# A two-layer decoder trunk on one core: SwiGLU's first stage by 256 gate and 256 up features, two steps of mLSTM's head 0 on other engines, and one early DMA on another queue

## The chip, the cores and the metric

The kernel runs on one core of a Trainium2 chip. The metric is the device time of one launch in microseconds (us). Before the change it is 825.69 us, the median of 3 runs (825.42 to 826.16). The engines are named as in the profile: PE multiplies matrices, DVE and POOL work elementwise, ACT copies, casts and evaluates functions, and SP issues DMAs (so does ACT's queue, for one of them).

## The reference, cut to what matters

256 tokens, model width 1024, two layers. Layer i is a token mixer (gMLP for layer 0, mLSTM with 4 heads of 512 for layer 1), then SwiGLU, then a sigmoid-gated embedding. All of it is float32.

```
def swiglu(x, w_gate, w_up, w_down):           # 1024 -> 2816 -> 1024
    return (jax.nn.silu(x @ w_gate) * (x @ w_up)) @ w_down

# mLSTM, per head: P = (q k^T) * decay weights, lower triangular; num = P v; den = sum P
h = layer_norm(num / max(|den|, exp(-m)), norm_g) + skip * xc
return (h * jax.nn.silu(z)) @ w_out

x = layer_norm(ALPHA * x + mixer(x), ln1_g[i], ln1_b[i])
x = layer_norm(ALPHA * x + swiglu(x, ...), ln2_g[i], ln2_b[i])
x = x + sigmoid(x @ ple_w_gate[i] + ple_b_gate[i]) * (p[i] @ ple_w_proj[i])
```

## The kernel before

**Weights and products.** The weights are streamed from HBM in tiles of 512 KB (`raw`, 4 buffers, issued by SP at L176). `split` (L153) makes of each a high part, a cast by ACT, and a low part, a subtraction by DVE. The two parts of a weight stand in a tile `w` (6 buffers) or, for the keys in `WIDE`, in a tile of the pool `b8` (8 buffers); those in `EARLY` are split some blocks ahead of their use. A product is three matmuls: high by high, high by low, low by high. A planner puts the instructions of each engine in an order of its own, and waits follow from the data; PSUM is used as two rings of four banks, A and B.

**SwiGLU** (`channel_mixer`). The 2816 hidden features are 22 blocks of 128. For blocks 0 to 3 the tokens are the stationary operand: `first(t)` (L537) fills, for token tile t of 128 tokens, one bank with 512 gate features and one with 512 up features, 24 matmuls of 512 columns each (16 at L286/L287, 8 at L289). ACT and DVE make `hn` of them (L552, L553), which `transpose_h` (L560) turns into feature order by four transposes a tile and splits into `hs`. Between the gate bank and the up bank of token tile 0 stand the eight transposes of the second token tile of x (`transpose_x(1)`, L326), after which ACT and DVE split `xs` for that tile. Blocks 4 to 21 go by `gate_up(f)` (L567): the weights are stationary, high matmuls take x's high and low part side by side (512 columns, L260), low ones 256 columns (L264). `down_blocks` says after which f which blocks are multiplied by the down weights (12 matmuls a block, `acc`, L240 to L242): 0 to 3 after f = 5, then one a step.

**mLSTM's heads.** P of a head (`sc`, 128 x 384, L917) is split in two: `phi` by ACT, `plo` by POOL (L920, with `sub=pool`). `pv_block` (L925) multiplies them by v (L937 to L939, L939 with `plo`) and sums P's rows (`pd`); DVE then takes the row scale and the statistics (`dn`, `hst`, `hmv`, `hrs`), POOL a power (L962), and ACT writes the normalised head `hn` (L967). `h_block` (L973) transposes it, adds the skip (L980), multiplies by silu(z) (`y*sz`, L981, DVE) and splits the result into `hs`. The output product `acc` starts with blocks 0 to 2 on token tile 0 (four banks A), then on token tile 1, whose banks are those that held head 3's `num` until L967 has read them.

**The start.** x arrives transposed, in four tiles `xr` (L359 to L368). The first half of the first tile is issued by ACT's queue, its second half by SP, between the two halves of the first weight tile (L178). The first six matmuls (L422) need the first half of `raw`, those after them the second, which ACT casts at L382.

Of the kernel before, what the change touches and what calls it, by code (L numbers as in the profile page):

```python
# [9 lines left out]
F32R = mybir.dt.float32r  # L10
# [4 lines left out]
P = 128  # L15
# [31 lines left out]

WIDE = {(n, l, k) for l in range(2) for n, m in (("g", 4), ("u", 2), ("pg", 6)) for k in range(m)}  # L50
EARLY = {("wo", 17 + k): ("g", 0, k) for k in range(4)}
EARLY |= {("mo", 8 + 2 * k): ("g", 1, k) for k in range(3)}
EARLY |= {("d", l, 10 + k): ("pg", l, k) for l in range(2) for k in range(6)}


def down_blocks(f):

    return range(4) if f == 3 + LAG else [f - LAG] if f > 3 + LAG else []

# [2 lines left out]

def stationary(key):

    return key[0] in ("u", "xm") and len(key) == 2 or key[0] in ("g", "u", "z") and key[-1] >= 4


def paired(key):  # L70

    return key[0] in ("g", "u") and len(key) == 3 and key[-1] >= 4 or key[0] == "u" and len(key) == 2


def weight_plan(a):
# [16 lines left out]

    def ffn(l):
        add(("pj", l, 0), a["ple_proj"][l, 0])
        for n in ("g", "u"):
            for kp in range(4):
                add((n, l, kp), a["ffn_" + n][l, kp])
        for f in range(4, NF + LAG):
            for n in ("g", "u") if f < NF else ():
                add((n, l, f), a["ffn_" + n][l, f])  # L100
# [33 lines left out]
def trunk(ctx, tc, a, out):  # L134
# [35 lines left out]
    def ahead(loads, casts):  # L170
        while at["load"] < min(len(plan), at["use"] + loads):
            ap = plan[at["load"]][1]
            n = ap.shape[-1]
            t = tl("raw", [P, n], name="raw")
            for c in HALF if at["load"] < 3 else [slice(0, n)]:
                at["dma"] = sp.dma_start(t[:, c], ap[:, c])  # L176
                if at["load"] == 0 and c.start == 0:
                    second_x()  # L178
            raws[at["load"]] = t
            at["load"] += 1  # L180
        while at["cast"] < min(len(plan), at["use"] + casts):
# [177 lines left out]
    for i in range(4):  # L359
        t = tl("m2", [P, 2, S], name="xr")  # L360
        if i == 0:

            act.dma_start(t[:, 0, :], a["xT"][i, :, 0, :])
            second_x = lambda: sp.dma_start(xr[0][:, 1, :], a["xT"][0, :, 1, :])
            xr.append(t)
        else:
            sp.dma_start(t, a["xT"][i])
            xr.append(t)  # L368
        ahead(1 + i, 0)
# [147 lines left out]
    def channel_mixer(l, acc, last, hook=None):  # L517
# [19 lines left out]

        fw = {}  # L540

        def first(t, between=lambda: None):
            ps = {}
            for n in ("g", "u"):
                if t == 0:
                    fw[n] = [weight(n, l, kp) for kp in range(4)]
                ps[n] = bank("B", [P, 512], "first")
                tok_from_x(ps[n], t, fw[n])
                if n == "g":
                    between()  # L550
            h = tl("m2", [P, 512], name="hn")
            act.activation(h, ps["g"], AF.Silu)  # L552
            dve.tensor_tensor(h, h, ps["u"], ALU.mult)  # L553
            return h

        hn = [first(0, lambda: transpose_x(1)), first(1)]
        hs = {e: tl("h", [P, 2, S], F32R, "h") for e in range(4)}

        def transpose_h(t):
            tp = bank("B", [P, 4, P], "tp")  # L560
            for e in range(4):
                pe.transpose(tp[:, e, :], hn[t][:, e * P:(e + 1) * P], ident)
            for e in range(4):
                split(hs[e][:, 0, TOK[t]], hs[e][:, 1, TOK[t]], tp[:, e, :])

        def gate_up(f):
# [20 lines left out]

        transpose_h(0)
        rows = []
        for f in range(4, NF + LAG):  # L590
            if f < NF:
                gate_up(f)
            if f == 4:
                transpose_h(1)
                acc = Down(NF)
            for e in down_blocks(f):
# [105 lines left out]
    def mlstm(embed1):  # L702
# [156 lines left out]
        with tc.manual_schedule(engines={mybir.EngineType.Activation}):  # L859
# [43 lines left out]
            for h in range(NH):  # L903
# [67 lines left out]
        def h_block(h):  # L971
            for j in range(2):
# [43 lines left out]
def lay_out(inputs):  # L1016
# [26 lines left out]
    def part(w):  # L1043
# [14 lines left out]
        "ffn_g": np.stack([mixed(w) for w in i["ffn_w_gate"]]),  # L1058
        "ffn_u": np.stack([mixed(w) for w in i["ffn_w_up"]]),
# [44 lines left out]
```

## Time and profile before

| what | value |
|---|---|
| median of 3 runs | 825.69 us |
| profiled execution, its own time | 825.63 us |
| its span | 823.9 us |
| PE busy | 816.9 us (99%) |
| DVE, ACT, POOL busy | 75%, 57%, 18% |
| granted TensorE clock | 1.00 of full speed |
| DMA read | 153.67 MB |

All times below are of the one profiled execution and count from the start of its span; 1.7 us of its time lie outside the span. The granted clock is 1.00 throughout, the level of 2.4 GHz. A row of the timeline gives the start, the duration, the engine, the line, the operation with the tiles it writes and reads, and, in brackets, how long the engine sat idle before it and what released it. Ends of PE's matmuls are modelled, so that the pace of PE is read from starts.

### The profile page before, as it was taken

To read this page: it belongs to the slowest core of one execution; us is meant where nothing else is said; L and a number is where in the kernel's file an instruction comes from. 1 tells how busy PE (TensorE), PEld (TensorE's weight loads), DVE (VectorE), ACT (ScalarE), POOL (GpSimd) and SP (SyncE) were. 2 spreads that over 40 slices of the span, in tenths; PEclk is the share of its full clock that TensorE was granted. 3 is DMA by queue.
4 is the path that set the end of the run, shared out by engine and by line. 5 is a ranking of instruction groups with operands and counts; after the bars stand their busy time and mean duration, and the time that the engine had idled before them with its cause. 6 is when DMAs were issued, how large, how long until landed. Compare 5 with 4: busy or idle time off the path is not lost.

```text
span 823.9 us, 12407 instructions
## 1 busy us (share of the span) xinstructions
PE 816.9 (99%) x4520; PEld 708.0 (86%) x4520; DVE 614.3 (75%) x982; ACT 470.9 (57%) x820; POOL 149.6 (18%) x209
## 2 busy tenths in 40 slices
PE   9999999999999999999999999999999999999997
PEld 6888888888888888888889999988888888888886
DVE  6757998678956567586878998889885656776674
ACT  6656666565535556475256788776444555665522
POOL 1020643342000000700001677330000000000000
PEclk9999999999999999999999999999999999999999
DMA  8895447567176678677144355454626667886501
GB/s 287 283 337 182 153 159 225 179 194 243 67 260 202 192 225 281 201 229 252 38 146 156 135 162 161 146 177 147 215 90 224 196 199 228 269 264 212 179 1 51
DMA packets 44997, 155.52 MB, mean 189 GB/s; under 512 B 5256, under 2 KB 6024, under 8 KB 44936
## 3 DMA queue, kind: packets, MB, share of 16 engines
q1 hardware_dynamic: 44792, 154.60, 57.6%
q8 instruction: 35, 0.57, 0.3%
q14 instruction: 26, 0.21, 0.1%
q10 hardware_dynamic: 144, 0.13, 0.0%
HBM read 153.67 MB, written 1.05 MB: 188 GB/s over the span
## 4 chain that ended last, share of the span: by engine, by line
PE 96%; DVE 1%; ACT 1%; DMA 1%; issue 0%; POOL 0%; SPq 0%; DVEq 0%; ACTq 0%
PE acc L240 9%; PE acc L241 9%; PE acc L242 9%; PE pu L260 8%; PE pg L260 8%; PE ups L260 5%; PE pg L264 4%; PE pu L264 4%; PE ups L264 3%; PE vps L242 2%; PE vps L240 2%; PE vps L241 2%; PE xmps L245 2%; PE xmps L247 2%; PE xmps L246 2%; PE gate L289 2%
## 5 line engine op out<-in xcount | busy, mean ns | idle before, releaser
L153 DVE TENSOR_TENSOR w<-raw,w 128x1024 fp32r<-128x1024 f32 (+1 forms) x275 | 333.2, 1219 | 74.7 <-ACT w L153 73.1
L153 ACT CAST w<-raw 128x1024 fp32r<-128x1024 f32 (+1 forms) x275 | 284.9, 1046 | 120.6 <-PE acc L242 25.7
L240 PE MATMUL acc<-w,h 128*128 128x512 f32 x336 | 133.0, 396 | 0.2 <-ACT hn L967 0.2
L241 PE MATMUL acc<-w,h 128*128 128x512 f32 x336 | 131.3, 391 | 0.0
L242 PE MATMUL acc<-w,h 128*128 128x512 f32 x336 | 131.0, 390 | 0.0
L242 PEld LDWEIGHTS acc<-w,h 128*128 128x128 f32 x336 | 63.1, 188 | 13.9
L240 PEld LDWEIGHTS acc<-w,h 128*128 128x128 f32 x336 | 63.1, 188 | 12.1 <-ACT hn L967 0.6
L241 PEld LDWEIGHTS acc<-w,h 128*128 128x128 f32 x336 | 63.1, 188 | 11.2 <-DVE h L153 0.2
L260 PE MATMUL pg<-xs,w 128*128 128x512 f32 x288 | 71.6, 391 | 0.0
L260 PE MATMUL pu<-xs,w 128*128 128x512 f32 x288 | 71.5, 390 | 0.0
L260 PEld LDWEIGHTS pg<-xs,w 128*128 128x128 f32 x288 | 53.8, 188 | 11.0
L260 PEld LDWEIGHTS pu<-xs,w 128*128 128x128 f32 x288 | 53.8, 188 | 11.0
L319 POOL TENSOR_TENSOR rs<-ve,mhalf 128x1 f32<-128x1 f32 x8 | 7.6, 956 | 295.9 <-DVE ve L318 291.3
L271 ACT COPY s<-pg 128x256 f32<-128x256 f32 x36 | 13.4, 372 | 69.7 <-PE pg L264 69.7
L260 PE MATMUL ups<-xs,w 128*128 128x512 f32 x192 | 47.9, 391 | 0.0
L272 DVE TENSOR_TENSOR s<-s,pg 128x256 f32<-128x256 f32 x36 | 15.1, 421 | 42.8 <-ACT s L271 42.7
L260 PEld LDWEIGHTS ups<-xs,w 128*128 128x128 f32 x192 | 35.7, 188 | 7.2
L264 PEld LDWEIGHTS pg<-xs,w 128*128 128x128 f32 x288 | 38.9, 188 | 3.1
L264 PE MATMUL pg<-xs,w 128*128 128x256 f32 x288 | 39.5, 280 | 0.0
L264 PE MATMUL pu<-xs,w 128*128 128x256 f32 x288 | 39.4, 279 | 0.0
L264 PEld LDWEIGHTS pu<-xs,w 128*128 128x128 f32 x288 | 36.5, 188 | 0.3
L245 PE MATMUL xmps<-xs,w 128*128 128x256 f32 x128 | 36.3, 284 | 0.0
(252 smaller groups left out, 1635.7 us busy)
## 6 DMA issues: line engine op xcount, KB each, us to landing
raw<-in_ffn_g SPq DMA_DIRECT2D x44, 512.0 KB, 4.4
raw<-in_ffn_u SPq DMA_DIRECT2D x44, 512.0 KB, 4.6
raw<-in_ffn_d SPq DMA_DIRECT2D x44, 512.0 KB, 4.3
raw<-in_gm_u SPq DMA_DIRECT2D x24, 512.0 KB, 3.5
raw<-in_gm_wo SPq DMA_DIRECT2D x24, 512.0 KB, 3.4
raw<-in_gm_v SPq DMA_DIRECT2D x21, 512.0 KB, 5.2
raw<-in_ple_gate SPq DMA_DIRECT2D x16, 512.0 KB, 4.5
raw<-in_ml_z SPq DMA_DIRECT2D x16, 512.0 KB, 3.8
```

Source lines behind the costliest of these rows:

```text
L153: return dve.tensor_copy(hi, src) if fast else act.copy(hi, src), sub.tensor_tensor(lo, src, hi.bitcast(F32), ALU.subtract)
L240: pe.matmul(ps, lh, w[:, 0, c], start=start, stop=False)
L241: pe.matmul(ps, ll, w[:, 0, c], start=False, stop=False)
L242: pe.matmul(ps, lh, w[:, 1, c], start=False, stop=stop)
L245: pe.matmul(ps, w[:, 0, c], h, start=start, stop=False)
L246: pe.matmul(ps, w[:, 0, c], l, start=False, stop=False)
L247: pe.matmul(ps, w[:, 1, c], h, start=False, stop=stop)
L260: pe.matmul(ps, w[:, 0, k * P:(k + 1) * P], xs[:, k], start=k == 0, stop=False)
L264: pe.matmul(ps[:, 0], w[:, 1, k * P:(k + 1) * P], xh[:, k, :], start=False, stop=k == KD - 1)
L271: act.copy(o, ps[:, 1])
L272: dve.tensor_tensor(o, o, ps[:, 0], ALU.add)
L289: pe.matmul(ps, xl[:, k, TOK[t]], w[:, 0, c], start=False, stop=k == KD - 1)
```

## The change

Five places change. (1) `first(t)` fills one bank with 256 gate and 256 up features, from four new weight tiles `f` per layer that hold both side by side; so it covers blocks 0 and 1, and `gate_up` takes 2 to 21. `transpose_x(1)` stands between the high matmuls and the low ones of token tile 0. (2) Down blocks 0 and 1 come together after f = 3, then one a step. (3) `plo` of head 0 is DVE's, those of heads 1 to 3 stay POOL's. (4) The gate `y*sz` of head 0's four blocks is POOL's, those of the other heads stay DVE's. (5) Both halves of x's first tile are issued by ACT's queue.

```diff
-WIDE = {(n, l, k) for l in range(2) for n, m in (("g", 4), ("u", 2), ("pg", 6)) for k in range(m)}
-EARLY = {("wo", 17 + k): ("g", 0, k) for k in range(4)}
-EARLY |= {("mo", 8 + 2 * k): ("g", 1, k) for k in range(3)}
+WIDE = {(n, l, k) for l in range(2) for n, m in (("f", 4), ("pg", 6)) for k in range(m)}
+EARLY = {("wo", 17 + k): ("f", 0, k) for k in range(4)}
+EARLY |= {("mo", 8 + 2 * k): ("f", 1, k) for k in range(4)}
...
 def down_blocks(f):
-    return range(4) if f == 3 + LAG else [f - LAG] if f > 3 + LAG else []
+    return range(2) if f == 1 + LAG else [f - LAG] if f > 1 + LAG else []
...
-                if at["load"] == 0 and c.start == 0:
-                    second_x()
...
-            act.dma_start(t[:, 0, :], a["xT"][i, :, 0, :])
-            second_x = lambda: sp.dma_start(xr[0][:, 1, :], a["xT"][0, :, 1, :])
+            for k in range(2):
+                act.dma_start(t[:, k, :], a["xT"][i, :, k, :])
...
-        def first(t, between=lambda: None):
-            ps = {}
-            for n in ("g", "u"):
-                if t == 0:
-                    fw[n] = [weight(n, l, kp) for kp in range(4)]
-                ps[n] = bank("B", [P, 512], "first")
-                tok_from_x(ps[n], t, fw[n])
-                if n == "g":
-                    between()
+        def first(t, before=(None, None)):
+            if t == 0:
+                fw.extend(weight("f", l, kp) for kp in range(4))
+            ps = bank("B", [P, 512], "first")
+            tok_from_x(ps, t, fw, before)
+            h = tl("m2", [P, 256], name="hn")
+            act.activation(h, ps[:, :256], AF.Silu)
+            dve.tensor_tensor(h, h, ps[:, 256:], ALU.mult)
...
-        hn = [first(0, lambda: transpose_x(1)), first(1)]
+        hn = [first(0, (0, lambda: transpose_x(1))), first(1)]
...
-        for f in range(4, NF + LAG):
+        for f in range(2, NF + LAG):
...
-                split(hi, lo, p, sub=pool)
+                split(hi, lo, p, sub=pool if h else dve)
...
-                    dve.tensor_tensor(y, y, sz[f // 8][:, f % 8, :], ALU.mult)
+                    (dve if h else pool).tensor_tensor(y, y, sz[f // 8][:, f % 8, :], ALU.mult)
```

PE in layer 0's first stage, from its last pair of high matmuls into `first` for token tile 0 to the first `gate_up`; before:

```order
L289 MATMUL first<-w,xs 128x512 x8
L326 MATMUL tp<-ident,xn_80 128x128 x8
L286 MATMUL first<-w,xs 128x512
L287 MATMUL first<-w,xs 128x512
...
L289 MATMUL first<-w,xs 128x512 x8
L562 MATMUL tp<-ident,hn 128x128 x4
L260 MATMUL pg<-xs,w 128x512 x8
```

and now:

```order
L323 MATMUL tp<-ident,xn_80 128x128 x8
L286 MATMUL first<-w,xs 128x512 x8
L283 MATMUL first<-w,xs 128x512
L284 MATMUL first<-w,xs 128x512
...
L286 MATMUL first<-w,xs 128x512 x8
L554 MATMUL tp<-ident,hn 128x128 x2
L257 MATMUL pg<-xs,w 128x512 x8
```

The transposes of x's second token tile stand ahead of the eight low matmuls of tile 0 (L289, now numbered L286), and two stages instead of four lie between x's transposes of tile 0 and `gate_up`.

DVE where mLSTM's heads begin (`sc` is P of a head, `gm` its decay weights, `w` the low part of a weight tile); before:

```order
L917 SCALAR_TENSOR_TENSOR sc<-sc,e 128x384
L909 TENSOR_TENSOR gm<-gb,cmask 128x256 x2
L153 TENSOR_TENSOR w<-raw,w 128x1024
L917 SCALAR_TENSOR_TENSOR sc<-sc,e 128x384
L153 TENSOR_TENSOR w<-raw,w 128x1024
```

and now:

```order
L909 SCALAR_TENSOR_TENSOR sc<-sc,e 128x384
L901 TENSOR_TENSOR gm<-gb,cmask 128x256 x2
L152 TENSOR_TENSOR plo<-sc,phi 128x384
L152 TENSOR_TENSOR w<-raw,w 128x1024
L909 SCALAR_TENSOR_TENSOR sc<-sc,e 128x384
L152 TENSOR_TENSOR w<-raw,w 128x1024 x2
```

Head 0's `plo` stands ahead of the first `w` on DVE, and head 1's P one instruction later.

DVE again, from head 0's skip sums (L980) to head 3's statistics; before:

```order
L980 SCALAR_TENSOR_TENSOR y<-tp,par,a_4149 128x256 x2
L981 TENSOR_TENSOR y<-y,sz 128x256
L153 TENSOR_TENSOR h<-y,h 128x256 x3
L981 TENSOR_TENSOR y<-y,sz 128x256
L949 SCALAR_TENSOR_TENSOR dn<-pd,cols 128x2
L153 TENSOR_TENSOR w<-raw,w 128x1024
L153 TENSOR_TENSOR h<-y,h 128x256
L950 TENSOR_TENSOR dn<-dn,pd 128x2
```

and now:

```order
L958 SCALAR_TENSOR_TENSOR nb<-hmv,hrs 128x2
L973 SCALAR_TENSOR_TENSOR y<-tp,par,a_4175 128x256 x4
L152 TENSOR_TENSOR w<-raw,w 128x1024
L152 TENSOR_TENSOR h<-y,h 128x256 x4
L942 SCALAR_TENSOR_TENSOR dn<-pd,cols 128x2
L943 TENSOR_TENSOR dn<-dn,pd 128x2
```

The four gates are gone from DVE; all four subtractions of `h`, which wait for POOL's gates by way of ACT's casts, now stand ahead of head 3's first `dn`. On POOL, after the power of head 2 and ahead of that of head 3, stand:

```order
L955 TENSOR_TENSOR hrs<-hrs,mhalf 128x2 x2
L975 TENSOR_TENSOR y<-y,sz 128x256 x4
L955 TENSOR_TENSOR hrs<-hrs,mhalf 128x2
L316 TENSOR_TENSOR rs<-ve,mhalf 128x1 x4
```

Before, the four powers (L962) followed each other there without the gates between.

## Rows read from the trace of the kernel before

**Rows 1.** The page, part 4: shares of the chain that ended last.

```profile
PE 96%; DVE 1%; ACT 1%; DMA 1%; issue 0%; POOL 0%; SPq 0%; DVEq 0%; ACTq 0%
```

**Rows 2.** The timeline of PE, layer 0's SwiGLU, first stage to block 6.

```profile
223.15 1.98 PE L289 MATMUL first<-w,xs 128*128 128x512 f32 x8
224.97 1.04 PE L326 MATMUL tp<-ident,xn 128*128 128x128 f32 x8
...
236.76 0.39 PE L286 MATMUL first<-w,xs 128*128 128x512 f32 x1
...
242.21 0.60 PE L562 MATMUL tp<-ident,hn 128*128 128x128 f32 x4
...
254.17 0.40 PE L240 MATMUL acc<-w,h 128*128 128x512 f32 x1
...
265.08 1.07 PE L260 MATMUL pg<-xs,w 128*128 128x512 f32 x4
...
273.32 0.84 PE L260 MATMUL pg<-xs,w 128*128 128x512 f32 x3
```

**Rows 3.** The timeline of DVE, then of ACT, around the same first stage.

```profile
222.37 0.75 DVE L344 SCALAR_TENSOR_TENSOR xn<-xn,rs,row 128x512 f32<-128x512 f32 x1
...
227.59 1.28 DVE L153 TENSOR_TENSOR xs<-tp,xs 128x512 fp32r<-128x512 f32 x2
...
214.07 1.05 ACT L153 CAST w<-raw 128x1024 fp32r<-128x1024 f32 x1 [3.51 <-DMA raw<-in_ffn_u]
217.47 0.59 ACT L524 COPY pp<-pps 128x512 f32<-128x512 f32 x1 [2.35 <-PE pps L242]
```

**Rows 4.** The timeline where mLSTM's heads begin, all engines, the rows that concern plo.

```profile
534.47 1.20 DVE L153 TENSOR_TENSOR w<-raw,w 128x1024 fp32r<-128x1024 f32 x1
534.50 2.04 POOL L153 TENSOR_TENSOR plo<-sc,phi 128x384 fp32r<-128x384 f32 x1 [11.40 <-ACT phi L153]
...
535.60 1.36 DVE L917 SCALAR_TENSOR_TENSOR sc<-sc,e 128x384 f32<-128x384 f32 x1
...
535.74 0.40 PE L938 MATMUL num<-vn,phi 128*128 128x512 f32 x1
...
536.60 0.50 PE L939 MATMUL num<-vn,plo 128*128 128x512 f32 x1 [0.47 <-POOL plo L153]
...
536.89 1.21 DVE L153 TENSOR_TENSOR w<-raw,w 128x1024 fp32r<-128x1024 f32 x1
...
537.59 1.39 POOL L153 TENSOR_TENSOR plo<-sc,phi 128x384 fp32r<-128x384 f32 x1 [1.04 <-ACT phi L153]
```

**Rows 5.** Line L981: its instructions; duration ns min/median/max, first and last start.

```profile
L981 DVE TENSOR_TENSOR y<-y,sz x16: 394/418/419, 555.0 to 588.8; 128x256 f32<-128x256 f32 x16
```

**Rows 6.** POOL's groups by line and form: busy us, mean ns.

```profile
L477 POOL TENSOR_TENSOR sv<-sv,cf 128x256 f32<-128x256 f32 x22 | 22.9, 1042 | 72.0 <-ACT sv L476 72.0
```

**Rows 7.** The timeline of DVE, ACT and PE from head 3's statistics to the output product.

```profile
560.39 0.15 DVE L951 RECIPROCAL dn<-dn 128x2 f32<-128x2 f32 x1
...
564.51 1.45 ACT L967 ACTIVATE hn<-num,nb,hrs 128x512 f32<-128x512 f32 x2 [0.75 <-DVE nb L965]
...
564.78 0.39 PE L242 MATMUL acc<-w,h 128*128 128x512 f32 x1
565.35 0.50 PE L240 MATMUL acc<-w,h 128*128 128x512 f32 x1 [0.18 <-ACT hn L967]
```

**Rows 8.** The timeline of the start: PE, ACT and DVE.

```profile
7.39 0.96 PE L422 MATMUL vps<-w,xs 128*128 128x512 f32 x3 [0.57 <-ACT w L382]
15.23 0.62 PE L242 MATMUL vps<-w,xs 128*128 128x512 f32 x2
...
6.72 0.62 ACT L382 CAST w<-raw 128x512 fp32r<-128x512 f32 x1 [1.44 <-DMA raw<-in_gm_v]
12.58 1.05 ACT L153 CAST w<-raw 128x1024 fp32r<-128x1024 f32 x1 [0.64 <-DMA raw<-in_gm_v]
...
13.66 2.47 DVE L153 TENSOR_TENSOR w<-raw,w 128x1024 fp32r<-128x1024 f32 x2 [0.87 <-ACT w L153]
```

More of the change, by code (lines that the diff above doesn't have):

```diff
@@ L45 @@
 Z_AFTER_XM = {1: 4, 5: 5, 10: 6, 15: 7}
-WIDE = {(n, l, k) for l in range(2) for n, m in (("g", 4), ("u", 2), ("pg", 6)) for k in range(m)}
-EARLY = {("wo", 17 + k): ("g", 0, k) for k in range(4)}
-EARLY |= {("mo", 8 + 2 * k): ("g", 1, k) for k in range(3)}
+WIDE = {(n, l, k) for l in range(2) for n, m in (("f", 4), ("pg", 6)) for k in range(m)}
+EARLY = {("wo", 17 + k): ("f", 0, k) for k in range(4)}
+EARLY |= {("mo", 8 + 2 * k): ("f", 1, k) for k in range(4)}
 EARLY |= {("d", l, 10 + k): ("pg", l, k) for l in range(2) for k in range(6)}
 def down_blocks(f):
-    return range(4) if f == 3 + LAG else [f - LAG] if f > 3 + LAG else []
+    return range(2) if f == 1 + LAG else [f - LAG] if f > 1 + LAG else []
 ASIDE = 56
 def stationary(key):
-    return key[0] in ("u", "xm") and len(key) == 2 or key[0] in ("g", "u", "z") and key[-1] >= 4
+    return key[0] in ("g", "u", "xm") or key[0] == "z" and key[-1] >= 4
 def paired(key):
-    return key[0] in ("g", "u") and len(key) == 3 and key[-1] >= 4 or key[0] == "u" and len(key) == 2
+    return key[0] in ("g", "u")
 def weight_plan(a):
@@ L94, in ffn @@
         add(("pj", l, 0), a["ple_proj"][l, 0])
-        for n in ("g", "u"):
-            for kp in range(4):
-                add((n, l, kp), a["ffn_" + n][l, kp])
-        for f in range(4, NF + LAG):
+        for kp in range(4):
+            add(("f", l, kp), a["ffn_f"][l, kp])
+        for f in range(2, NF + LAG):
             for n in ("g", "u") if f < NF else ():
-                add((n, l, f), a["ffn_" + n][l, f])
+                add((n, l, f), a["ffn_" + n][l, f - 2])
             for e in down_blocks(f):
@@ L536, in channel_mixer @@
         boundary(0, g1, b1)
-        fw = {}
-        def first(t, between=lambda: None):
-            ps = {}
-            for n in ("g", "u"):
-                if t == 0:
-                    fw[n] = [weight(n, l, kp) for kp in range(4)]
-                ps[n] = bank("B", [P, 512], "first")
-                tok_from_x(ps[n], t, fw[n])
-                if n == "g":
-                    between()
-            h = tl("m2", [P, 512], name="hn")
-            act.activation(h, ps["g"], AF.Silu)
-            dve.tensor_tensor(h, h, ps["u"], ALU.mult)
-            return h
-        hn = [first(0, lambda: transpose_x(1)), first(1)]
-        hs = {e: tl("h", [P, 2, S], F32R, "h") for e in range(4)}
+        fw = []
+        def first(t, before=(None, None)):
[6 more added lines that the diff above has]
+            dve.tensor_tensor(h, h, ps[:, 256:], ALU.mult)
+            return h
+        hn = [first(0, (0, lambda: transpose_x(1))), first(1)]
+        hs = {e: tl("h", [P, 2, S], F32R, "h") for e in range(2)}
         def transpose_h(t):
-            tp = bank("B", [P, 4, P], "tp")
-            for e in range(4):
+            tp = bank("B", [P, 2, P], "tp")
+            for e in range(2):
                 pe.transpose(tp[:, e, :], hn[t][:, e * P:(e + 1) * P], ident)
-            for e in range(4):
+            for e in range(2):
                 split(hs[e][:, 0, TOK[t]], hs[e][:, 1, TOK[t]], tp[:, e, :])
@@ L589, in channel_mixer @@
         rows = []
-        for f in range(4, NF + LAG):
+        for f in range(2, NF + LAG):
             if f < NF:
                 gate_up(f)
-            if f == 4:
+            if f == 2:
                 transpose_h(1)
@@ L1057, in lay_out @@
         "gm_gb": np.stack([i["gm_ln_g"][0], i["gm_ln_b"][0]], 1).reshape(NU, P, 2).transpose(1, 0, 2),
-        "ffn_g": np.stack([mixed(w) for w in i["ffn_w_gate"]]),
-        "ffn_u": np.stack([mixed(w) for w in i["ffn_w_up"]]),
+        "ffn_f": np.stack([
+            tok(np.concatenate([g[:, :256], u[:, :256]], 1))[0] for g, u in zip(i["ffn_w_gate"], i["ffn_w_up"])
+        ]),
+        "ffn_g": np.stack([feat(w[:, 256:]) for w in i["ffn_w_gate"]]),
+        "ffn_u": np.stack([feat(w[:, 256:]) for w in i["ffn_w_up"]]),
         "ffn_d": i["ffn_w_down"].reshape(2, NF, P, D),
```

## The prediction

> **What bounds the kernel now.** I read first the chain that ended last, by engine: PE holds 96% of it [rows 1], so an edit counts where it takes matmuls off PE or closes a wait of PE. Then the timeline of PE in layer 0's SwiGLU, where the reader is to see matmuls of 512 columns starting every 0.227 us: eight from 223.15 to 224.97 [rows 2]. Then the waits of PE that lie where the change is: 0.47 us for `plo` at 536.60 [rows 4], 0.18 for `hn` at 565.35 [rows 7], 0.57 for the cast of the first weight's second half at 7.39 [rows 8]. Idle time is counted from a modelled end; the loss is the distance of two starts less 0.227.
>
> **SwiGLU.** Per layer two of the four token-tile stages go. One is 242.21 - 236.76 = 5.45 us [rows 2], so 10.90. Four of the eight transposes of `hn` go: eight took 1.04 and four 0.60 [rows 2], 0.11 each, 0.4 together. Two blocks of `gate_up` come. From block 6 to block 7 it is 273.32 - 265.08 = 8.24, with one down block in it; four down blocks are 265.08 - 254.17 = 10.91, 2.73 each [rows 2]; so a `gate_up` is 5.51 and two are 11.02. The down blocks stay 22. Per layer 11.02 - 10.90 - 0.4 = -0.28; I take -0.25 for the first `gate_up`'s start-up, -0.5 for both layers, with ends of -0.8 and 0 (the latter if the waits below cost 0.25 a layer).
>
> What must hide: the transposes of x's second token tile now stand where the eight low matmuls began, at 223.15. Their last operand is written by DVE at 222.37 + 0.75 = 223.12 [rows 3], just in time; the first four read the half written earlier. The 0.79 or so that they take passes to ahead of the low matmuls, nothing is added. ACT then has until about 223.15 + 0.8 + 1.8 = 225.8 for the high part of `xs`. DVE's low part is needed by the second tile's own low matmuls, 16 x 0.227 = 3.6 later, at 229.4; it is written by 227.59 + 1.28 = 228.87 behind four weight subtractions [rows 3], a number that doesn't change. The slack is 0.5. If the cover is gone, PE waits what is missing, once a layer. The weights of blocks 2 and 3 are four tiles, split between the first tiles and x's second half; before, these were the up tiles 0 to 3, of which two were split ahead of `pp`; now all four are (the fourth rival).
>
> **Head 0's `plo`.** POOL takes it from 534.50 to 536.54; PE's matmul with it starts at 536.60, 0.86 after the one before it at 535.74 [rows 4]. Without the wait it is 0.23, of which a little may come from the restart; the loss is 0.63, with 0.11 for the slower restart 0.74. On DVE a subtraction of 256 columns is 0.42 [rows 5] and one of 1024 columns 1.20 [rows 4], so 384 columns lie at about 0.55. DVE begins at 534.47, where `w` began, and ends at 535.02, ahead of 535.74 + 0.23 = 535.97, where PE wants it. So the wait goes whole: -0.74. What is behind it on DVE: `w`, 0.55 later, and head 1's P, which now finds no POOL in its way. Nothing near them made PE wait.
>
> **Head 0's gates, and head 3.** POOL's four gates lengthen a chain that ends in the next wait. PE reaches the second token tile of the output product at 564.78 + 0.23 = 565.01 and starts at 565.35 [rows 7], since ACT reads head 3's banks until 564.51 + 0.77; the loss is 0.34 and 0.10 of restart. With `plo`'s wait gone PE comes at 564.27. In the new order head 3's `dn` stands behind four subtractions of `h`, these behind ACT's casts, these behind POOL's gates. From `dn`'s reciprocal at 560.39 to the end of ACT's first read at 565.28 it was 4.9 [rows 7]; with the two operations ahead of the reciprocal 5.1 from the start of `dn`, and the one DVE gate that stood in it pays for the skip sum that now does. The skip sums move up with the two weight subtractions around them, to about 553.8 (they follow head 2's statistics; ends 553.4 and 554.5, an estimate from the order and these durations), and the first gate can start at 554.3.
>
> How long four gates take on POOL no row shows. Bound below: DVE's own queue. Four skip sums (about 0.43 each, like the gates of the same size, 1.7), `w` (1.2) and four subtractions (1.5) from 553.8 end at 558.2, and `hn` at 563.3: no wait, -0.74 - 0.44 = -1.18. The nearest row is POOL's sum of two SBUF tiles of the same 128 x 256, 1.04 us on average over 22 [rows 6]: four are 4.2, to 558.5; a cast and a subtraction (0.41 each) to 559.3, `hn` at 564.4, PE 0.2 late: -0.74 - 0.2 = about -0.9. Bound above: a gate stands still while DVE runs an instruction with two SBUF inputs, and the reverse. That this happens is in the rows: `w` runs from 534.47 to 535.67, `plo` ends 0.87 later, and P, begun at 535.60, takes 1.36, to 536.96; head 1's `plo` ends at 538.98, 0.88 after the `w` that ended at 538.10 [rows 4]. Then the third gate waits for `w`, the fourth alternates with the subtractions of `h`, the last of which ends at 560.0, `hn` at 565.1 and PE 0.9 late: -0.15, and with the later start +0.55. I take -0.6 for `plo` and gates together, nearer to the row than to the bound, and keep -1.18 and +0.55. The Trainium skill ("SBUF — State Buffer", section "Who interferes with whom") says that a DVE instruction with two SBUF inputs and a POOL instruction that reads SBUF exclude each other for whole instructions. By that rule the upper bound is the sum, and head 0's gates undo what `plo` gains; the trace agrees with it, by the 0.87 and 0.88 above.
>
> **The start.** The loss at 7.39 is 0.57 + 0.39 - 0.23 = 0.73, with the restart 0.85. It waited for ACT's cast at 6.72, and that for the second half of the first weight tile [rows 8], which now is issued one place earlier. But what PE gains here it must keep. The fourth weight tile landed at 12.56, ACT cast it from 12.58, DVE subtracted it from 13.66, the first by 14.9, and PE used it at 15.23 [rows 8]: 0.25 of slack. If the bytes ahead of that tile, which are the same, take as long, no more than 0.25 can be kept. I take -0.2; ends -0.85 (all landings earlier) and +0.2 (the second half of x interleaves with the first weight half and delays both). The Trainium skill ("DMA: Bandwidth & Descriptors", section "Issuing engines are not separate DMA queues") says that DMAs of all issuing engines run on the same 16 engines, and that issuing from two saves only the issue time. By it the gain is the 0.25 and not the 0.85; the trace of before has no run to show it.
>
> One more wait on ACT, POOL and DVE: ACT casts weights one or two places earlier in several stretches; each of those tiles was ready with ACT idle, so nothing is charged.
>
> **Sum.** -0.5 - 0.6 - 0.2 = -1.3, so 825.63 - 1.3 = 824.3 in the profiled execution's terms. That execution stands 0.06 under the median of the runs, which is nothing here: I predict 824.3. What a measurement of this kernel can tell from no change is 0.2%, 1.65 us; so faster means under 824.04, and slower over 827.34.
>
> **Rivals.**
> More is gained: either POOL's gates run free and head 3's wait goes too, -0.5 - 1.18 - 0.2 = 823.75, or the start keeps its whole 0.85, -0.5 - 0.6 - 0.85 = 823.7; with both, 823.1. For: head 3's chain has 0.9 us of room between the free case and PE. Against: the 1.04 of rows 6, and the tile at 12.56.
> The gates are locked out and the start gives nothing: -0.5 + 0.2 - 0.1 = 825.2. For: the two cases of rows 4. Against: DVE runs skip sums, which read one SBUF tile and PSUM, in half of the gates' time.
> `plo` on DVE is still late (DVE not free at 534.47, since the planner's order is not a time), and nothing else moves there: -0.5 - 0 - 0.2 = 824.9. Against: half a microsecond of slack.
> Slower: ACT's order in both layers now has five weight casts ahead of `pp` and of `xs`, the last for a tile that is issued just before the stage. A cast that waits for its landing holds `pp`, `xs` and so PE's first stage. Before, the corresponding tile landed at 214.04 and `pp` was wanted at 217.47 [rows 3]. With a cast (1.05) ahead of `pp`, PE waits when the landing comes after about 217.3, us for us. To come out 0.2% slower it has to cost 1.65 + 1.3 = 2.95, 1.5 a layer: a landing at 218.8. At 219 in both layers the time is 824.3 + 3.4 = 827.7. For: `raw` has four buffers, so the tile can't be issued before its fourth predecessor is split, and nothing on ACT can pass the cast that waits for it. Against: 3.3 us of room.
>
> **Chances.** The forecast 0.45, with its own range 823.6 to 825.0; more gained 0.28; locked out 0.12; `plo` late 0.07; slower 0.08. Under 824.04 lie a third of the forecast (0.15), most of the second (0.22) and little else: faster 0.37. Slower is the last, 0.08. The rest, 0.55, is the same. The range leaves out that last case and the tails of both ends, one in ten above and below: 823.1 to 825.9.
>
> **What would show it.** In SwiGLU: a first stage of two banks, and from the end of its first sixteen matmuls (223.15) to the start of `gate_up` 6 (265.08) 41.7 us instead of 41.9, with no idle time of PE at the transposes of x's second tile nor 3.6 us into tile 1. At head 0: `plo` on DVE near 0.55 and no wait at the third matmul. At head 3: POOL's gates at 0.75 to 1.0 each; where they reach 1.2 or more and `hn` ends after 564.9 on this clock, the term is wrong. At the start: no wait at the seventh matmul, and one in its place before 15.2. The prediction is wrong if PE waits in SwiGLU, if the landings of the first 13 us shift as a whole, or if the waits that go turn up in a place that no row here names.

## The result, and the profile after

The changed kernel takes 827.12 us, the median of 20 executions (825.65 to 829.5), against 825.62 before (20 executions, 824.88 to 826.24). The ratio is 1.0018, with a 95% interval of 1.0012 to 1.0025: slower by 1.0 to 2.1 us, where 1.3 less was forecast. The profiled execution takes 826.53, its span is 824.7.

Where the time went is read from four starts of PE that both kernels have, taken from their timelines: the first `pps` matmul of layer 0 (before SwiGLU), the first `num` matmul of head 0, the first `pps` matmul of layer 1, and the last matmul.

| stretch | before | after | difference |
|---|---|---|---|
| start and gMLP, to `pps` of layer 0 | 215.91 | 214.93 | -0.97 |
| with SwiGLU of layer 0, to head 0's `num` | 319.61 | 319.36 | -0.25 |
| mLSTM's heads and output, to `pps` of layer 1 | 70.56 | 72.97 | +2.41 |
| with SwiGLU of layer 1, to the last matmul | 213.23 | 212.84 | -0.39 |

So all of the loss stands in 73 us of mLSTM. The page's chain by engine shows it as DVE, 3% where it was 1% [rows 1]:

```profile
PE 94%; DVE 3%; ACT 1%; issue 1%; DMA 1%; POOL 0%; DVEq 0%; ACTq 0%; POOLq 0%
```

The view of waits of PE (engine, line, what it waited for: total us, times, longest) names two in this stretch, neither of them `plo`:

```profile
PE acc L237 <- ACT hn L960: 2.2, 1, 2.2
PE num L930 <- ACT e L904: 0.9, 1, 0.9
```

**SwiGLU** went as worked out. In the timeline of PE the transposes of x's second token tile start at 222.21, the low matmuls 0.79 later, the second tile at 224.91, 8 x 0.227 + 0.09 on; PE doesn't idle there [rows 2]:

```profile
222.21 1.03 PE L323 MATMUL tp<-ident,xn 128*128 128x128 f32 x8
223.00 2.07 PE L286 MATMUL first<-w,xs 128*128 128x512 f32 x8
224.91 0.39 PE L283 MATMUL first<-w,xs 128*128 128x512 f32 x1
...
230.36 0.38 PE L554 MATMUL tp<-ident,hn 128*128 128x128 f32 x2
...
263.84 1.98 PE L257 MATMUL pg<-xs,w 128*128 128x512 f32 x8
```

From the transposes, where the sixteen high matmuls end, to `gate_up` 6 it is 41.63 us; it was 41.93. DVE's low part of `xs` is done at 225.91 + 1.28 = 227.19, ahead of 224.91 + 3.63 = 228.5 [rows 3].

**The start**, in this execution, kept more than forecast: PE runs its first 24 matmuls in one piece, and ACT casts the fourth weight tile 0.94 us earlier [rows 8]:

```profile
4.85 5.90 PE L418 MATMUL vps<-w,xs 128*128 128x512 f32 x24
...
11.64 1.05 ACT L152 CAST w<-raw 128x1024 fp32r<-128x1024 f32 x1 [0.62 <-DMA raw<-in_gm_v]
```

**mLSTM.** `plo` of head 0 on DVE takes 0.55 us and PE doesn't wait for it [rows 4]. Then ACT, in the planner's new order, casts two weight tiles ahead of head 1's P. P is ready at 535.40; ACT waits for the landings of both tiles, 1.11 and 0.24 us, and casts P at 537.77, 2.4 us late. The timeline of DVE, then of ACT:

```profile
533.24 0.55 DVE L152 TENSOR_TENSOR plo<-sc,phi 128x384 fp32r<-128x384 f32 x1
533.71 1.21 DVE L152 TENSOR_TENSOR w<-raw,w 128x1024 fp32r<-128x1024 f32 x1
534.85 0.55 DVE L909 SCALAR_TENSOR_TENSOR sc<-sc,e 128x384 f32<-128x384 f32 x1
...
535.53 1.05 ACT L152 CAST w<-raw 128x1024 fp32r<-128x1024 f32 x1 [1.11 <-DMA raw<-in_ml_wo]
536.82 1.06 ACT L152 CAST w<-raw 128x1024 fp32r<-128x1024 f32 x1 [0.24 <-DMA raw<-in_ml_wo]
537.77 0.51 ACT L152 CAST phi<-sc 128x384 fp32r<-128x384 f32 x1
```

The later steps of the heads hang on that cast: `plo` of head 1 on POOL, P of head 2 on DVE, its cast, head 3's decay weights, and with them the bank that head 1's second `num` needs. PE waits there 1.02 us beyond its pace, between 540.33 and 541.58, and 2.34 at `hn`, between 563.29 and 565.86 [rows 7]. The timeline of POOL, DVE and PE:

```profile
538.36 1.65 POOL L152 TENSOR_TENSOR plo<-sc,phi 128x384 fp32r<-128x384 f32 x1 [16.48 <-ACT phi L152]
541.04 0.99 POOL L152 TENSOR_TENSOR plo<-sc,phi 128x384 fp32r<-128x384 f32 x1 [1.04 <-ACT phi L152]
...
555.81 3.99 POOL L975 TENSOR_TENSOR y<-y,sz 128x256 f32<-128x256 f32 x4 [0.86 <-DVE y L973]
...
539.17 1.25 DVE L909 SCALAR_TENSOR_TENSOR sc<-sc,e 128x384 f32<-128x384 f32 x1
...
541.24 0.82 DVE L946 TENSOR_TENSOR dn<-dn 128x2 f32<-128x2 f32 x1
...
540.33 0.39 PE L932 MATMUL num<-vn,plo 128*128 128x512 f32 x1
541.58 0.50 PE L930 MATMUL num<-vn,phi 128*128 128x512 f32 x1 [0.86 <-ACT e L904]
...
563.29 0.39 PE L239 MATMUL acc<-w,h 128*128 128x512 f32 x1
565.86 0.50 PE L237 MATMUL acc<-w,h 128*128 128x512 f32 x1 [2.18 <-ACT hn L960]
```

The gates took 1.0 us each, as the row of the same size had it [rows 6]. They started at 555.81 and not at 554.3, although PE was 1.2 us ahead when the heads began. PE also came to the wait with 18 matmuls of the output product done, not 21, so that 0.68 us of work that had stood ahead of it now stood behind.

The account of mLSTM: -0.74 (no wait at `plo`), +1.02 and 0.11 of restart (head 1's `num`), and 2.34 - 0.34 = +2.0 (`hn`), together +2.4. The same from the end alone: after its wait at `hn` PE goes on when ACT has read the first of head 3's banks. Counted from head 0's first `num` that is 1.74 us later than before (31.52 against 29.78), and three matmuls more come behind it, 0.68: 2.42. What PE saved or lost ahead of that wait doesn't enter.

The median is worse than the profiled execution for one more reason. 7 of the 20 executions show a mean granted clock of 0.997 or 0.998 and take 828.1 us on average; the other 13 take 826.6. What may happen in them is seen in the trace of no_gate, below.

### The profile page after: what moved, and what is told of

Its sections match the earlier page's. It is cut to its first block, busy times and chain, and to the rows that moved or that the text cites. A ratio compares the mean times of both kernels' runs of the same rounds, so it can differ in the third digit from the quotient of the medians.

```text
span 824.7 us, 12477 instructions
## 1 busy us (share of the span) xinstructions
PE 816.1 (99%) x4544; PEld 708.6 (86%) x4544; DVE 618.2 (75%) x987; ACT 472.6 (57%) x828; POOL 152.5 (18%) x212
## 4 chain that ended last, share of the span: by engine, by line
PE 94%; DVE 3%; ACT 1%; issue 1%; DMA 1%; POOL 0%; DVEq 0%; ACTq 0%; POOLq 0%
PE acc L237 9%; PE acc L238 9%; PE acc L239 9%; PE pu L257 9%; PE pg L257 9%; PE ups L257 5%; PE pg L261 5%; PE pu L261 5%; PE ups L261 3%; PE vps L239 2%; PE vps L238 2%; PE vps L237 2%; PE xmps L242 2%; PE xmps L244 2%; PE xmps L243 2%; PE gate L286 2%
## 5 line engine op out<-in xcount | busy, mean ns | idle before, releaser
L257 PE MATMUL pg<-xs,w 128*128 128x512 f32 x320 | 79.5, 391 | 0.0
L257 PE MATMUL pu<-xs,w 128*128 128x512 f32 x320 | 79.4, 390 | 0.0
L257 PEld LDWEIGHTS pu<-xs,w 128*128 128x128 f32 x320 | 59.8, 188 | 12.3
L257 PEld LDWEIGHTS pg<-xs,w 128*128 128x128 f32 x320 | 59.8, 188 | 12.3
L269 DVE TENSOR_TENSOR s<-s,pg 128x256 f32<-128x256 f32 x40 | 16.8, 420 | 63.1 <-ACT s L268 63.1
L261 PEld LDWEIGHTS pg<-xs,w 128*128 128x128 f32 x320 | 43.2, 188 | 3.4
L261 PE MATMUL pg<-xs,w 128*128 128x256 f32 x320 | 43.9, 280 | 0.0
L261 PE MATMUL pu<-xs,w 128*128 128x256 f32 x320 | 43.7, 279 | 0.0
L261 PEld LDWEIGHTS pu<-xs,w 128*128 128x128 f32 x320 | 40.6, 188 | 0.3
```

The lines of the kernel that those rows point to most:

```text
L257: pe.matmul(ps, w[:, 0, k * P:(k + 1) * P], xs[:, k], start=k == 0, stop=False)
L261: pe.matmul(ps[:, 0], w[:, 1, k * P:(k + 1) * P], xh[:, k, :], start=False, stop=k == KD - 1)
L269: dve.tensor_tensor(o, o, ps[:, 0], ALU.add)
```

## The experiments

Each kernel was timed in five rounds against the kernel before. The table's last column is the distance from the first `pps` matmul of layer 0 to that of layer 1 in the profiled execution: SwiGLU of layer 0 and mLSTM, without the start. In no_gate and held it holds 1.6 and 1.4 us of matmuls at the lower clock (below), in the other traces none in mLSTM.

| kernel | median us | ratio (95%) | `pps` to `pps` us |
|---|---|---|---|
| before | 825.4 to 825.7 | 1 | 390.17 |
| changed | 827.12 | 1.0018 (1.0012 to 1.0025) | 392.33 |
| ffn | 824.86 | 0.9994 (0.9985 to 1.0003) | 389.92 |
| start | 825.46 | 0.9998 (0.9989 to 1.0007) | 390.15 |
| ffn_start | 824.62 | 0.9989 (0.9980 to 0.9997) | 389.93 |
| no_plo | 825.03 | 0.9995 (0.9986 to 1.0004) | 390.33 |
| no_gate | 828.03 | 1.0029 (1.0019 to 1.0040) | 393.08 |
| held | 827.58 | 1.0021 (1.0012 to 1.0030) | 393.24 |
| plo_order | 826.34 | 1.0012 (1.0003 to 1.0021) | 391.37 |
| fill | 826.42 | 1.0013 (1.0004 to 1.0022) | 392.62 |
| plo_free | 824.74 | 0.9988 (0.9979 to 0.9997) | 390.00 |
| plo_free_b4 | 824.16 | 0.9982 (0.9973 to 0.9991) | 389.56 |
| ng_b5 | 824.89 | 0.9994 (0.9985 to 1.0002) | 390.25 |
| hn_b5 | 824.64 | 0.9987 (0.9978 to 0.9996) | 390.69 |
| z_b5 | 824.61 | 0.9986 (0.9977 to 0.9994) | 390.38 |
| fs_b4 | 823.93 | 0.9980 (0.9971 to 0.9989) | 389.45 |

**Which part loses.** ffn_start takes both edits in mLSTM back, no_gate and no_plo one each:

```diff
-                split(hi, lo, p, sub=pool if h else dve)            # ffn_start, no_plo
+                split(hi, lo, p, sub=pool)
-                    (dve if h else pool).tensor_tensor(y, y, sz[f // 8][:, f % 8, :], ALU.mult)  # ffn_start, no_gate
+                    dve.tensor_tensor(y, y, sz[f // 8][:, f % 8, :], ALU.mult)
```

> The change without its two edits in mLSTM: plo of head 0 is POOL's again and its gates are DVE's. In the trace of the changed kernel PE is 0.97 us ahead after the start, 0.25 more after layer 0's SwiGLU and 0.36 more after layer 1's, and loses 2.4 us in mLSTM. Both theories (the loss comes from the weight casts that the planner moved when plo went to DVE; the loss comes from the gates on POOL) expect 825.6 - 1.6 = 824.0 us here, with mLSTM's two waits of before unchanged (about 0.5 us at plo, 0.2 at hn). A third, that the SwiGLU edit itself delays mLSTM's weights, expects more than 825.

> The change with head 0's gates back on DVE; plo stays on DVE. Theory 1 (casts): the planner's order has two weight casts ahead of ACT's cast of head 1's P here too, PE waits about 1 us at head 1's num again, the chain behind it is late, and the wait at hn stays above 1 us: 824.0 - 0.74 + 1.1 + 0.6 to 1.2 = 825.0 to 825.6. Theory 2 (gates): the wait at hn goes with the gates, below 0.3 us: 824.0 - 0.74 + 1.1 - 0.3 = 824.1 or less.

> The change with head 0's plo back on POOL; the gates stay on POOL. Theory 1 (casts): without the moved casts there is no wait at head 1's num, and the gates alone cost little: 824.0 to 824.4, wait at hn below 0.7. Theory 2 (gates): the wait at hn is 2 us or more, 826.0.

ffn_start gains 0.8 (824.62), 0.6 short of what was expected; mLSTM is as before in it, with the old waits. no_plo adds 0.4 to that, no_gate 3.4. So it is `plo` on DVE that loses, and the gates are a small matter: with `plo` on POOL they cost 0.4. With it on DVE the medians (827.12 against 828.03) can't be compared as they stand, since six of no_gate's seven executions have a mean clock of 0.998 or less, and 7 of 20 of the changed kernel; those with it take 828.1 in both, those without 825.85 (one) and 826.6. Theory 2 falls. Theory 1 named the right edit, and missed twice: no_gate is 2.4 above its range, and its trace waits 0.2 at head 1's `num`, not about 1. For the time the trace shows most of the reason, and 0.6 is ffn_start's own miss, by which no_plo too lies above its range. In the timeline of PE, the matmuls after the long wait start 0.427 us apart, the pace of the 1.2 GHz level, for 3.4 us, and then 0.227 again:

```profile
563.00 0.39 PE L239 MATMUL acc<-w,h 128*128 128x512 f32 x1
565.53 0.64 PE L237 MATMUL acc<-w,h 128*128 128x512 f32 x1 [2.14 <-ACT hn L960]
565.97 0.63 PE L238 MATMUL acc<-w,h 128*128 128x512 f32 x1
566.40 0.63 PE L239 MATMUL acc<-w,h 128*128 128x512 f32 x1
...
568.53 0.63 PE L238 MATMUL acc<-w,h 128*128 128x512 f32 x1
568.96 0.48 PE L239 MATMUL acc<-w,h 128*128 128x512 f32 x1
569.28 0.40 PE L237 MATMUL acc<-w,h 128*128 128x512 f32 x1
569.51 0.39 PE L238 MATMUL acc<-w,h 128*128 128x512 f32 x1
```

Eight steps of 0.2 are 1.6 us.

**Is it the clock.** fill gives PE work in that wait:

```diff
                     for t in range(2) if f == 2 else ():
+                        if t == 1:
+                            fps = bank("B", [P, 512], "fill")
+                            for i in range(8):
+                                end = pe.matmul(fps, begin[2][1][:, 0, TOK[0]], begin[2][2][:, 0, HALF[0]], start=True, stop=True)
+                        with issue_after((end,) if t else ()):
```

> no_gate with eight matmuls more, of 512 columns, whose result nobody reads, between the output product's first token tile and its second, where PE waits 2.1 us for hn; eight take 1.8 us. Theory 1 (part of no_gate's loss is that PE runs at half clock after the wait: starts 0.427 us apart from 565.5 on): the slow matmuls go, and the time is 826.0 to 826.6 instead of 828.0. Rival (the granted clock there is chance and has nothing to do with the wait): slow matmuls remain in some runs, 828 as before, or 829 if the eight are not covered.

826.42, against 828.03: as theory 1 had it. None of its executions has a clock under 0.999, and its trace has no matmul at the slow pace. The wait at `hn` shrinks to what the eight leave:

```profile
PE num L930 <- ACT e L904: 1.0, 1, 1.0
PE acc L237 <- ACT hn L960: 0.3, 1, 0.3
```

The matmuls do nothing for the result; PE only isn't idle. So 1.6 us of no_gate's loss is the clock after the wait. The rest is that wait's end, 0.9 later than before, and the three matmuls behind it.

**Is it the order of the casts.** held asks for one weight tile fewer ahead of head 1's P and for one behind it; plo_order (gates on DVE) holds the casts that z blocks 12 and 13 ask for behind P of heads 1 and 2.

```diff
-            feat_from_x(ps, weight("z", f, casts=2 if f > 10 else None), between)    # held
+            feat_from_x(ps, weight("z", f, casts=1 if f == 11 else 2 if f > 10 else None), between)
...
+                phi = split(hi, lo, p, sub=pool if h else dve)[0]    # held
+                if h == 1:
+                    behind["cast"] = (phi,)
+                    ahead(LOAD_AHEAD - 1, 1)
...
+            if h < 2:                                               # plo_order
+                behind["cast"] = (phis[1 + h],)
             z_act(*z_mm(12 + h))
```

> The whole change, but the second of the two weight tiles that ACT cast ahead of head 1's P is asked for behind that cast. Theory 1 (casts): no wait at head 1's num, no wait at plo, the wait at hn 0 to 0.5: 824.0 - 0.74 - 0.4 to 0 = 822.9 to 823.3, faster than every other run. Theory 2 (gates): the wait at hn is still about 2 us: 824.0 - 0.74 + 2.0 = 825.3.

> The change without the gates on POOL (as no_gate), but the weight casts that the z blocks 12 and 13 ask for are held until ACT has cast P of head 1 and of head 2; this puts the weight work behind the P of all heads on ACT and DVE, much as in the kernel before. Theory 1 (it was the order that came with plo on DVE): no wait at plo nor at head 1's num, the wait at hn below 0.6, and 824.6 (ffn_start) - 0.74 + 0.2 = about 824.0. Rival (DVE's chain of the four heads ends at the same time whatever PE does, so that plo's wait was covered by the wait at hn): the wait at hn is 1 us or more, and 824.4 to 825.2.

Neither has a wait at head 1's `num`, as theory 1 expected, and neither is faster than before: 827.58 and 826.34, both outside every range that was expected of them. The wait that is gone says little, since no_gate with the casts in place has only 0.2 of it. In held PE waits 2.7 us at `hn`. In plo_order the view of waits has 1.6 us in three places, two of them for weights, whose casts and subtractions now come late:

```profile
PE acc L237 <- ACT w L152: 0.6, 1, 0.6
PE acc L237 <- ACT hn L960: 0.5, 1, 0.5
PE acc L239 <- DVE w L152: 0.5, 1, 0.5
```

So holding the casts back brings head 1's P early, and not head 3's `hn`: by the table in the next section it ends at 31.33 and 30.22, against 29.78 before. In held POOL's gates are likely part of it, 5.5 us from the first start to the last end; hn_b5, without them and with five blocks, ends there at 30.46. What else holds the chain in these two orders is not shown.

**What the wait at `plo` was worth.** plo_free leaves head 0's `plo` out altogether and uses `phi` again, so that part of the product is wrong, no engine has more to do, and every engine keeps the order of ffn_start.

```diff
+                if h == 0:
+                    act.copy(hi, p)
+                    lo = hi
```

> ffn_start, but head 0's plo isn't computed at all: its matmul takes phi a second time, so that part of the product is wrong. All engines keep the order of the kernel before, and no work is added anywhere: the edit at its very best. As the prediction had it, the wait at plo is worth 0.74 and the wait at hn does not grow: 824.6 - 0.74 = 823.9 or less. Theory (the chain of the four heads on DVE ends when it ends, and PE's earlier arrival is waited out at hn): the wait at hn grows from 0.34 to 0.9 to 1.1, and the time is 824.4 to 824.7.

It takes 824.74, against 824.62 of ffn_start; against the runs of the kernel before beside each, 0.9 and 0.8 less. The 0.74 isn't there. In PE's timeline the nine `num` matmuls of head 0 run without a gap, 0.42 instead of 0.12 us pass ahead of head 2's first `num`, and the wait at `hn`, 0.18 of idle time before [rows 7], is 0.58:

```profile
545.88 0.28 PE L244 MATMUL zps<-xs,w 128*128 128x256 f32 x1
546.30 0.50 PE L933 MATMUL num<-vn,phi 128*128 128x512 f32 x1
...
563.84 0.39 PE L239 MATMUL acc<-w,h 128*128 128x512 f32 x1
564.81 0.50 PE L237 MATMUL acc<-w,h 128*128 128x512 f32 x1 [0.58 <-ACT hn L963]
```

The 0.74 that PE no longer waits at 535 it waits later: 0.4 at head 2's `num` and 0.4 more at `hn`, with their restarts. The wait of the prediction's second term was covered by the wait of its third.

**Work for PE in its place.** fs_b4 is ffn_start with four blocks instead of three for the first token tile ahead of the second; plo_free_b4 is the same on plo_free. ng_b5 and hn_b5 take five blocks on no_gate and on held with the gates on DVE. z_b5 is ffn_start with five blocks and z block 12 ahead of head 0's `num`.

```diff
-                if f < 3:
+                if f < 4:                                            # 5 in *_b5
-                    for t in range(2) if f == 2 else ():
+                    for t in range(2) if f == 3 else ():
...
+            z = z_mm(12) if h == 0 else None                         # z_b5
             pv_block(h)
-            z_act(*z_mm(12 + h))
+            z_act(*(z or z_mm(12 + h)))
```

> ffn_start (mLSTM as before) with four blocks instead of three multiplied for the first token tile before PE turns to the second, whose banks head 3's hn frees: 1.4 us more of work ahead of the wait at hn. Theory (the chain of the four heads on DVE and ACT ends by itself, and PE only has to have other work until then): the wait at hn (0.34, 0.1 of restart) goes and nothing comes in its place, 824.6 - 0.4 = 824.2. Rival (what is asked for earlier, the fourth block of h and the fourth weight tile, is late itself): a wait at an acc matmul for h or w, 824.6 or more.

> no_gate (plo of head 0 on DVE, in the planner's order) with five blocks for the first token tile before the second: 30 matmuls, 2.7 us more of work ahead of the wait at hn, which was 2.1 us there. Theory (the loss at hn is a chain that doesn't come earlier with PE, plus the half clock after the wait): both go, the wait at head 1's num (1.0) stays, plo's wait is gone: 824.6 - 0.74 + 1.1 - 0.4 = 824.5, against 828.0 of no_gate, and no slow matmuls. Rival (the order has made all of DVE's and ACT's work late, weights and h too): waits for h or w in its place, 825.5 to 826.5.

> held with head 0's gates back on DVE and five blocks for the first token tile: no wait at plo, none at head 1's num, and work in place of the wait at hn. Theory (all that plo on DVE cost was waits of PE for the chain, which other work of PE can fill): 824.6 - 0.74 - 0.44 = 823.4. Rival (late h or weights take the place of the wait): 824.5 or more.

> plo_free (head 0's plo not computed, phi in its place) with four blocks for the first token tile ahead of the second. Theory: the 1.36 us of other work cover the wait at hn, and only now the 0.74 come out: 823.93 (fs_b4) - 0.74 = 823.2. Rival (PE is held by h or by weights in this stretch anyway): 823.6 or more.

> The whole computation: ffn_start with PE's z block 12 ahead of head 0's num, so that POOL has its plo ready without any work being moved to DVE, and with five blocks for the first token tile ahead of the second. Theory: no wait at plo, and the later start of the chain is covered by the five blocks: 823.93 - 0.74 = 823.2, faster than every version so far. Rival (head 0's statistics come 2.8 us later and the chain with them): a wait at tp or hn of 1 us or more, 824 to 825.

fs_b4 takes 823.93, 0.3 below its expectation and the fastest of all kernels here: the one wait of PE left in mLSTM is the one at `plo`:

```profile
PE num L932 <- POOL plo L152: 0.5, 1, 0.5
```

plo_free_b4 takes 824.16: with `hn`'s wait covered, the missing `plo` still gains nothing. The rival's time holds, with another reason for most of it. Start for start against fs_b4, PE gives back 0.6 us at head 2's `num`, where it waits for head 0's `hn`, and 0.2 at an `acc` matmul. ng_b5 (824.89, expected 824.5) has no wait at `hn`, none at head 1's `num` and no slow matmuls, and new waits of 0.5 and 0.3 at head 2's transposes, which five blocks need early; hn_b5 (824.64, expected 823.4) has 0.6 there and 0.4 for a weight, its rival's case. Moving z block 12 moved the wait too (824.61, expected 823.2): no wait at `plo`, and 1.45 at head 2's `num`, for the banks that head 0's `hn` reads:

```profile
545.47 0.28 PE L244 MATMUL zps<-xs,w 128*128 128x256 f32 x1
547.19 0.50 PE L930 MATMUL num<-vn,phi 128*128 128x512 f32 x1 [1.45 <-ACT hn L960]
```

**The two parts by themselves.** ffn and start are the kernel before with one edit each, as in the diff of the change.

> The kernel before with the SwiGLU edit alone. By the working of the prediction 0.5 less (0 to 0.8), by the landmarks of the changed kernel's trace 0.25 + 0.36 = 0.6 less: 824.8. If the SwiGLU edit were not worth that, ffn_start's gain of 0.8 would be the start's, and this run would be at 825.4.

> The kernel before with one edit, x's first tile by ACT's queue alone. Theory 1, all landings come earlier and are kept: 0.7 to 1.0 us less than before, 824.5. Theory 2, the landings come earlier but the first matmuls run at half clock (as the starts 0.427 us apart at 5.6 to 6.5 us in two of the runs so far show), which takes back three steps of 0.2 us: 0.2 to 0.5 less, 825.0. Theory 3, as predicted, the landings are the same and 0.25 is kept: also about 825.2, but then the cast of the fourth weight tile starts at 12.6 as before and not at 11.6.

ffn is 0.64 faster than the runs beside it (825.50), its interval reaching just past none; in the traces of the kernels with the SwiGLU edit the stretch with layer 0's SwiGLU is 319.32 to 319.40 us (z_b5 aside, where a z block stands ahead of the first `num`), without it 319.61, and the last stretch 212.83 to 212.87 against 213.23. start is 0.04 faster, which is none: none of its theories. Its landings do come earlier (ACT casts the fourth weight tile at 12.17, against 12.58), though not by the same amount each time: over the traces of kernels with this edit that cast starts between 11.60 and 12.55. The first `vps` matmuls run at the slow pace in many traces, ffn's among them, which lacks the edit. With the edit the first `pps` matmul stands between 214.93 and 215.99, without it at 215.91 and 216.73. One trace can't size this term; what becomes of the earlier landings in most executions stays open.

## Why the prediction was wrong

**SwiGLU, -0.5.** Right in its mechanism and its size: -0.25 and -0.39 in the trace, 0.64 less timed alone. The cover at x's second tile held.

**The start, -0.2.** The reasoning was wrong: its limit of 0.25 took the landing of the fourth weight tile as fixed, and the landings did move. The median was within what was allowed: timed alone it is nothing, and ffn_start is 0.1 to 0.2 below ffn, inside the noise. The profiled execution's 0.97 is the best that was seen, and more than the prediction's end of 0.85; one of its own signs of being wrong, landings of the first 13 us that shift as a whole, came true.

**Head 0's `plo`, -0.74.** This is the step that failed. The prediction read PE's wait as a loss by itself: "So the wait goes whole: -0.74", and "Nothing near them made PE wait". It knew the next wait, at `hn`, and let its chain start earlier with PE ("The skip sums move up"). plo_free shows that the chain doesn't: with the wait taken away at no cost, nothing is gained. The trace shows where the chain is held. In ACT's order, that of the kernel before, a weight cast stands ahead of the cast of head 1's P, and waits for its landing. The timeline of DVE, then of ACT, in plo_free:

```profile
534.96 0.54 DVE L909 SCALAR_TENSOR_TENSOR sc<-sc,e 128x384 f32<-128x384 f32 x1
537.10 1.23 DVE L152 TENSOR_TENSOR w<-raw,w 128x1024 fp32r<-128x1024 f32 x1 [1.60 <-ACT w L152]
...
536.02 1.05 ACT L152 CAST w<-raw 128x1024 fp32r<-128x1024 f32 x1 [1.02 <-DMA raw<-in_ml_wo]
536.97 0.50 ACT L152 CAST phi<-sc 128x384 fp32r<-128x384 f32 x1
```

P is ready at 535.50, 0.8 earlier than in ffn_start counted from head 0's first `num`, and ACT takes it 0.3 later. DVE isn't what holds the chain at this place: busy 5.93 of 6 us in the kernel before, it is busy 4.40 in plo_free and stands idle for 1.60 until ACT has cast that weight, by the view by stretches (PE, PEld, DVE, ACT and POOL busy, the clock, the DMA's share, GB/s), before and then plo_free:

```profile
534.00:540.00 6.00, 5.54 (x39) 4.79 (x38) 5.93 (x9) 5.51 (x14) 3.43 (x2) 1.00 0.91 325
...
534.00:540.00 6.00, 6.00 (x45) 5.61 (x45) 4.40 (x7) 4.59 (x12) 1.65 (x1) 1.00 0.84 296
```

Whether plo_free gains in an execution whose tile lands earlier, no trace here shows.

**"ACT casts weights one or two places earlier in several stretches; each of those tiles was ready with ACT idle, so nothing is charged."** This failed too, and it is the larger part of the loss in mLSTM. ACT now has two weight casts ahead of head 1's P, and the tiles hadn't landed; in the kernel before it was one, and its tile had landed when ACT came to it, at 535.59. no_gate and fill have the same order there, and the landing differs between their traces: ACT waits 0.27 us for the first tile in no_gate and 1.41 in fill. The timeline of ACT, no_gate and then fill:

```profile
535.23 1.05 ACT L152 CAST w<-raw 128x1024 fp32r<-128x1024 f32 x1 [0.27 <-DMA raw<-in_ml_wo]
537.49 0.51 ACT L152 CAST phi<-sc 128x384 fp32r<-128x384 f32 x1
...
535.90 1.05 ACT L152 CAST w<-raw 128x1024 fp32r<-128x1024 f32 x1 [1.41 <-DMA raw<-in_ml_wo]
538.14 0.51 ACT L152 CAST phi<-sc 128x384 fp32r<-128x384 f32 x1
```

In the table are ends from the timelines, in us from each trace's first `num` of head 0: P of head 1 as DVE writes it, its cast by ACT, and ACT's first read of head 3's banks, after which PE goes on.

| kernel | P written | P cast | head 3's bank read | cast to read |
|---|---|---|---|---|
| before | 1.45 | 2.00 | 29.78 | 27.8 |
| ffn_start | 1.45 | 2.28 | 29.77 | 27.5 |
| plo_free | 0.62 | 2.60 | 29.88 | 27.3 |
| changed | 1.10 | 3.99 | 31.52 | 27.5 |
| no_gate | 1.11 | 3.17 | 30.65 | 27.5 |
| fill | 1.11 | 4.29 | 31.77 | 27.5 |
| held | 0.61 | 1.16 | 31.33 | 30.2 |
| plo_order | 0.64 | 1.19 | 30.22 | 29.0 |

Where the weight casts stand ahead of P, head 3's bank follows P's cast by 27.3 to 27.8 us: against ffn_start the changed kernel's cast is 1.71 later and its bank 1.75. Of the 1.71, 1.29 is the wait and the cast of the second tile, which the new order put there, and the rest the first tile's later landing in this execution. Held behind P, the same weight work makes the chain late in another way. The order was looked at for where instructions stood, and not for when their tiles land once ACT gets to them earlier.

**Head 3's chain.** The prediction bounded `plo` and gates together by +0.55, which without the -0.74 is +1.29 for this wait; it came to +2.0. POOL's gates are not why: they took 4.0 us, the middle case, no_plo puts them at 0.4, and from P's cast to head 3's bank it is 27.5 us with them (changed) and without (no_gate). What was late was their start, 1.5 us on the trace's clock, by the chain above; and the bound left out that the planner could put three matmuls behind the wait, 0.68.

**The rivals.** "Locked out", at 825.2, named the right place with another cause. "Slower" had the mechanism, a weight cast that waits for its landing and holds what stands behind it on ACT, and put it in SwiGLU, where it didn't happen; it happened at head 1's P. That a wait of 2.3 us is followed by matmuls at half clock was in no case; it is likely why the median is 0.6 above the profiled execution, and why the time is spread over 3.9 us where it was 1.4.

The exclusion of DVE and POOL showed again: `dn`, 128 x 2, takes 0.82 us where its neighbours take 0.16, while POOL's `plo` runs from 541.04. The Trainium skill ("SBUF — State Buffer", section "Who interferes with whom") says that a DVE instruction with two SBUF inputs contends with a POOL instruction that reads SBUF, and the trace agrees with it here. It isn't what lost the 2.4 us.

## What to carry to other kernels

A wait of the bounding engine is worth what it costs only if the next wait downstream moves with it. Before pricing it, follow the chain that feeds the next wait back to what starts it: here that was a cast on ACT, behind weight casts that wait for their landings. Where the chain doesn't move, independent work for the bounding engine at that next wait is the cheaper try (fs_b4: 823.93, by one constant more); here the earlier wait was worth nothing even then (plo_free_b4: 824.16). An edit that a planner sees can cost more by the order it brings than by its own work, and a wait of two microseconds on TensorE can have a tail after it.

## What the runs showed of the hardware

After a wait of PE of 2.3 to 2.9 us in mid-kernel (2.30 in no_gate, 2.86 in held, by starts) the matmuls ran at the pace of the 1.2 GHz level in the traces of no_gate and held, eight and six steps of about 0.43 us; after 2.34 us in the trace of the changed kernel they didn't. A mean granted clock of 0.997 or 0.998, which those two traces have, shows in some executions of one and the same kernel and not in others: 7 of 20 of the changed kernel, 6 of 7 of no_gate, 6 of 11 of held (and 1 of 11 of plo_order, whose waits are shorter). Those executions took 828.1 us on average in these three kernels, the others 826.6, 825.85 and 826.0. With eight matmuls of 1.8 us in the wait (fill) it happened in none of 11. The same slow pace shows at the first `vps` matmuls of several traces, one to four steps of 0.43 us; what that costs in the median is not shown.

The landing of one and the same weight tile differs between executions: ACT's idle time for the first `ml_wo` tile ahead of head 1's P was 0.27 us in no_gate, 1.11 in the changed kernel and 1.41 in fill, all with the same casts in the same order.
